# The second unit of each feed forward layer computed plain, in the other four PSUM banks, with its post-processing written behind the next unit

## The chip, the cores and the metric

The kernel runs on one core of a Trainium2 chip. The metric is the device time of one execution in microseconds, the median of three runs. Beside it stands the profile of one execution, taken by the hardware profiler; its span runs from the first to the last instruction.

## What is computed

One decoder layer on a residual x of 256 tokens by 2048 columns, in float32: half a SwiGLU layer, a mixer with two branches, half a second SwiGLU layer. Only the first and third steps are changed:

```python
def swiglu(h, w_gu, w_down):
    g, u = jnp.split(h @ w_gu, 2, axis=-1)
    return (jax.nn.silu(g) * u) @ w_down

x = x + 0.5 * swiglu(rms_norm(x, g_ffn1[l]), w_gu1[l], w_down1[l])
x = x + hybrid_mixer(rms_norm(x, g_mix[l]), ...)
x = x + 0.5 * swiglu(rms_norm(x, g_ffn2[l]), w_gu2[l], w_down2[l])
```

`w_gu` is 2048 by 11264 (5632 gate and 5632 up columns), `w_down` 5632 by 2048.

## The kernel before

**Split arithmetic.** Each float32 operand is held as two fp32r tiles, `hi` and `lo`, and a product is three matmuls: x hi by w hi, x hi by w lo, x lo by w hi. `split` makes the pair: ScalarE copies to `hi` (L98), VectorE subtracts to get `lo` (L99).

**Units.** A feed forward layer goes through its 11 units of 512 gate and 512 up columns in blocks of 4, 4 and 3 (`UNITS`). Behind each block its activations are multiplied with `w_down` in four column chunks (`dn`, n = 0 to 3, function `by_token`). A *plain* unit has 16 parts, one for each 128 rows of the weights; a part is 4 products (gate and up, two token halves of 128), which is 12 matmuls of 128x512. The other units follow `PLAN = "sppspspp"`: the 16 row blocks are taken as 8 pairs, and for an "s" pair the 8 products are replaced by 7 (Strassen's scheme in Winograd's form, `seven`), which come in four parts and need sums of the weights (`u`, L167 to L169, on VectorE), and sums of the activations, the *forms*. Three "s" pairs a unit save 9 matmuls out of 192.

**Normalisation.** The first unit works on x times the gains; each token's factor `rstd` is applied at the end (`direct`: ScalarE's silu with scale, L486, here called the *gate*, and VectorE's multiplication, L490, the *up*). The forms need activations that are normalised. `turn_into_forms` does that in place for one pair: L315 and L316 on VectorE, four small operations L320 to L323 if the pair is an "s", then a split back into `h` (L98, L99). Each FFN needs 8 such *turns*. The split back on ScalarE has to wait until TensorE has read the old `h`.

**PSUM.** There are eight banks: `ps_mm` has two tiles of two banks each, `ps_t` two tiles of one (tag "tr"), `ps_a` two of one ("sc", "po"). A plain unit has its four accumulators in `ps_mm`. A unit by plan has four of its accumulators there, and p5, p7, p6 and p1 in the other four banks. After the last "s" pair `gather` reads these four, and at the unit's end `combine` (L476 to L479) reads the two `ps_mm` tiles. A `dn` chunk takes one `ps_mm` tile; its `add` (L562) reads it into x.

**Order of the work.** All engines work in the order in which the program is written. `Feed.take` gives the next weight part and first writes the splits of the parts ahead: three pairs of buffers for any part, and two more from the pool `late` for parts of units whose plan is given. `pending` holds small steps, one of which is written behind each part; `posts` holds steps that are written at the end of a `take`, one each, or three when five are queued. `turns` are the transposes of a unit's activations (`transpose4`, into `ps_t`), then split into `act`. In the first FFN `NormOfColumns` computes the statistics from `xT` during unit 0: squares on ScalarE (`stats`, L350), their sum on GpSimd (L352), `sums`, `total`, `spread`, all put into `pending` by `start1`.

Behind the mixer stands the product with `w_o` in four chunks (`o`, `by_token`), whose `add` is L835, and which feeds the second FFN.

Of the kernel before, what the change touches and what calls it, by code (L numbers as in the profile page):

```python
# [12 lines left out]
F32 = mybir.dt.float32  # L13
F32R = mybir.dt.float32r
AF = mybir.ActivationFunctionType
# [4 lines left out]
P = 128  # L20
D = 2048
S = 256
TB = S // P
NKD = D // P
DFF = 5632
UNITS = (4, 4, 3)
PAIRS = NKD // 2
PLAN = "sppspspp"
HD = 64
NQ = 16  # L30
NKV = 4
# [9 lines left out]
NCH = 512  # L41
# [11 lines left out]
def hybrid_layer(ctx: ExitStack, tc: tile.TileContext, a: dict, out: bass.AP):  # L53
# [47 lines left out]
    def halves(cat, k0, k1):  # L101
        return cat[:, k0:k1, 0], cat[:, k0:k1, 1]

    def transpose4(srcs, name):

        pt = ps_t.tile([P, 2, S], F32, tag="tr", name=name)
# [9 lines left out]
    def run(queue, n=1):  # L116
        for _ in range(min(n, len(queue))):
            queue.pop(0)()
# [271 lines left out]
    def add_ffn(w_gu, w_down, first=None):  # L390
        u0 = 0
        for units in UNITS:
            for u in range(u0, u0 + units):
                hooks = dict(plan=PLAN if u else None)
                if first and u == 0:
                    cuts = [NCH, NCH] + [SUB] * 7
                    hooks = dict(cuts=cuts, on_fetch=first.fetch, on_split=first.parts)
# [17 lines left out]
    class Unit:  # L415


        def __init__(self, norm, fpool, late_pool):
            self.norm, self.fpool, self.pool = norm, fpool, late_pool
            self.begun = set()  # L420
            self.banks = {}

        def bank(self, name):

            if name in ("a0", "a1", "b0", "b1"):
                if name[0] not in self.banks:
                    self.banks[name[0]] = ps_mm.tile([P, 2, NCH], F32, tag="mm", name="gu")
                return self.banks[name[0]][:, int(name[1])]
            if name not in self.banks:
                pool, tag = dict(p1=(ps_t, "tr"), p6=(ps_t, "tr"), p5=(ps_a, "sc"), p7=(ps_a, "po"))[name]  # L430
                self.banks[name] = pool.tile([P, NCH], F32, tag=tag, name=name)
            return self.banks[name]
# [49 lines left out]

        def direct(self):
            g = self.g = self.fpool.tile([P, TB, NCH], F32, tag="g", name="g", bufs=2)
            for t in range(TB):
                nc.scalar.activation(  # L486
                    g[:, t], self.banks["ab"[t]][:, 0], AF.Silu, scale=self.norm.rstd[:, t:t + 1]
                )
            for t in range(TB):
                nc.vector.scalar_tensor_tensor(  # L490
                    g[:, t], self.banks["ab"[t]][:, 1], self.norm.rstd[:, t:t + 1], g[:, t],
                    op0=ALU.mult, op1=ALU.mult,
                )

        def turns(self, act, k):

            def turn(j):
                pt = transpose4([self.g[:, t, 2 * P * j:2 * P * (j + 1)] for t in range(TB)], "at")
                posts.append(lambda: split(halves(act, k + 2 * j, k + 2 * j + 2), pt))

            return [lambda j=j: turn(j) for j in range(UKT // 2)]

    def ffn(norm, fpool, open_late, first=None, after=None, late=(), out_rows=None):
        late_pool = None if first else open_late()
        n_unit = 0
        for i, units in enumerate(UNITS):
# [1 line left out]
            act = fpool.tile([P, max(UNITS) * UKT, 2, S], F32R, tag="act", name="act")  # L508
            turns = []
            for u in range(units):  # L510
                unit = Unit(norm, fpool, late_pool)
                if n_unit == 0:
                    end = NKD * SUB
                    if first:
                        first()
                    col = w = 0
                    while col + w < end:
                        hi, lo, w, col = feed.take()
                        unit.plain(hi, lo, w, col, col + w == end)
                        run(pending)  # L520
                        if first and col + w == end - 2 * SUB:
                            late_pool = unit.pool = open_late()
                        if norm.spread_done and late_pool and 2 * (norm.turned + 1) * SUB <= col + w:
                            norm.turn_into_forms(norm.turned, late_pool)
                            norm.turned += 1
                    run(posts, len(posts))
                    unit.direct()
                else:
                    for p in range(PAIRS):
                        if norm.turned <= p:  # L530
                            norm.turn_into_forms(norm.turned, late_pool)
                            norm.turned += 1
                        if PLAN[p] == "s":
                            unit.seven(p, "s" not in PLAN[p + 1:])
                            if "s" not in PLAN[p + 1:]:
                                unit.gather()
                            continue
                        for j in range(2):
                            hi, lo, w, col = feed.take()
                            unit.plain(hi, lo, w, col, p == PAIRS - 1 and j == 1)  # L540
                            run(pending)
                            if norm.turned < PAIRS:
                                norm.turn_into_forms(norm.turned, late_pool)
                                norm.turned += 1
                            if p == PAIRS - 1 and j == 0:
                                run(turns, len(turns))
                    run(posts, len(posts))
                    unit.combine()
                run(turns, len(turns))
                turns = unit.turns(act, u * UKT)  # L550
                n_unit += 1
                if late:
                    late.pop(0)()
            pending.extend([lambda: None] * 2 + turns)
            for n in range(ND):
# [28 lines left out]
    with tc.tile_pool(name="ffn1", bufs=1) as fpool, ExitStack() as early, ExitStack() as later:  # L584
# [33 lines left out]
    with tc.tile_pool(name="mix", bufs=1) as mix:  # L618
# [300 lines left out]
```

## Time and profile before

| | |
|---|---|
| median of 3 runs | 2131.32 us (2130.17 to 2131.93) |
| profiled execution, its own time | 2131.02 us |
| its span | 2129.2 us |
| TensorE (matmul) busy | 2067.4 us, 97% |
| VectorE busy | 1513.2 us, 71% |
| ScalarE busy | 1027.3 us, 48% |
| GpSimd busy | 64.3 us, 3% |
| mean granted TensorE clock | 0.991 of full speed |

The busy time of TensorE is modelled from pipelined matmuls, so that 97% does not say that the array is at its peak. What counts is where matmuls don't follow each other: most of the span TensorE is busy without a break, and its breaks lie at the beginnings of the two feed forward layers and at the ends of blocks. Time outside the span is 1.8 us.

### The profile page before, as it was taken

The numbers are of one execution on the slowest core, as the hardware profiler recorded it, in microseconds if no ns is written. First come the engines' busy times: TensorE is split into PE (matmuls) and PEld (weight loads), VectorE is DVE, ScalarE is ACT, GpSimd is POOL, SyncE is SP. The second block draws the span as 40 slices with busy tenths as digits, with TensorE's granted clock in tenths as the row PEclk, the third lists the DMA queues.
The fourth block names the chain that finished last, engine by engine and source line by source line (L and its number), as shares of the span: only waits on it lengthen the run. The fifth ranks groups of instructions, "written<-read, shape, count | busy, mean of one in ns | idle before, by whom it ended". The sixth has DMA issues, their size and how long they took to land.

```text
span 2129.2 us, 24288 instructions
## 1 busy us (share of the span) xinstructions
PE 2067.4 (97%) x9560; PEld 1687.9 (79%) x9560; DVE 1513.2 (71%) x1669; ACT 1027.3 (48%) x1234; POOL 64.3 (3%) x55
## 2 busy tenths in 40 slices
PE   8799999999999999999999999979999999999999
PEld 7578778887788788877888888757878778787777
DVE  5888568885688654668666665588965888648874
ACT  5454445543455454455545444445543555434543
POOL 1000000000000000621000000000000000000000
PEclk9899999999999999999999999999999999999999
DMA  6355555554555455443555555434555545555454
GB/s 242 124 190 215 178 198 199 190 205 158 198 197 199 168 183 186 160 152 113 184 197 181 195 187 189 178 127 170 198 181 194 198 178 199 190 187 195 183 193 158
DMA packets 57939, 389.68 MB, mean 183 GB/s; under 512 B 6880, under 2 KB 8032, under 8 KB 11744
## 3 DMA queue, kind: packets, MB, share of 16 engines
q1 hardware_dynamic: 57680, 388.10, 50.2%
q8 instruction: 75, 1.23, 0.2%
q14 instruction: 40, 0.33, 0.0%
q10 hardware_dynamic: 144, 0.02, 0.0%
HBM read 386.00 MB, written 2.10 MB: 182 GB/s over the span
## 4 chain that ended last, share of the span: by engine, by line
PE 88%; DVE 6%; ACT 2%; issue 2%; POOL 1%; DMA 1%; SPq 0%; ACTq 0%; DVEq 0%; POOLq 0%
PE gu L437 10%; PE gu L438 10%; PE gu L436 10%; PE dn L221 8%; PE dn L223 8%; PE dn L222 7%; PE gate L243 5%; DVE lo L99 3%; PE yo L243 3%; PE gate L245 3%; PE p L436 2%; PE p L437 2%; PE p L438 2%; PE xc L243 2%; ACT hi L98 2%
## 5 line engine op out<-in xcount | busy, mean ns | idle before, releaser
L99 DVE TENSOR_TENSOR lo<-raw,hi 128x1024 fp32r<-128x1024 f32 (+1 forms) x729 | 868.6, 1203 | 525.0 <-ACT hi L98 517.5
L98 ACT CAST hi<-raw 128x1024 fp32r<-128x1024 f32 (+1 forms) x729 | 728.0, 1012 | 631.9 <-PE dn L223 253.0
L436 PE MATMUL gu<-hi,h 128*128 128x512 f32 x1048 | 418.7, 399 | 29.2 <-DVE g L490 8.1
L437 PE MATMUL gu<-lo,h 128*128 128x512 f32 x1048 | 417.3, 398 | 9.0 <-DVE lo L99 8.2
L438 PE MATMUL gu<-hi,h 128*128 128x512 f32 x1048 | 414.3, 395 | 0.0
L221 PE MATMUL dn<-hi,act 128*128 128x512 f32 x704 | 278.7, 396 | 8.8 <-DVE v L477 8.8
L223 PE MATMUL dn<-hi,act 128*128 128x512 f32 x704 | 276.2, 392 | 0.0
L222 PE MATMUL dn<-lo,act 128*128 128x512 f32 x704 | 273.8, 389 | 0.0
L436 PEld LDWEIGHTS gu<-hi,h 128*128 128x128 f32 x1048 | 198.9, 190 | 84.6 <-issue 12.8
L437 PEld LDWEIGHTS gu<-lo,h 128*128 128x128 f32 x1048 | 198.9, 190 | 61.7 <-DVE lo L99 19.4
L98 ACT CAST hi<-u 128x1024 fp32r<-128x1024 f32 x120 | 126.2, 1052 | 229.7 <-DVE u L167 183.2
L438 PEld LDWEIGHTS gu<-hi,h 128*128 128x128 f32 x1048 | 198.9, 190 | 45.1 <-DVE h L285 0.8
L243 PE MATMUL gate<-h,hi 128*128 128x512 f32 x512 | 179.2, 392 | 0.0
L221 PEld LDWEIGHTS dn<-hi,act 128*128 128x128 f32 x704 | 132.3, 188 | 37.4 <-issue 11.2
L223 PEld LDWEIGHTS dn<-hi,act 128*128 128x128 f32 x704 | 132.2, 188 | 30.2
L222 PEld LDWEIGHTS dn<-lo,act 128*128 128x128 f32 x704 | 132.2, 188 | 28.8
L99 DVE TENSOR_TENSOR lo<-u,hi 128x1024 fp32r<-128x1024 f32 x120 | 146.5, 1222 | 3.4 <-ACT hi L98 0.3
L245 PE MATMUL gate<-h,lo 128*128 128x256 f32 x480 | 134.4, 280 | 0.0
L243 PEld LDWEIGHTS gate<-h,hi 128*128 128x128 f32 x512 | 95.9, 187 | 20.6 <-issue 0.8
L243 PE MATMUL xc<-h,hi 128*128 128x512 f32 x256 | 93.4, 407 | 0.0
L245 PEld LDWEIGHTS gate<-h,lo 128*128 128x128 f32 x480 | 90.7, 189 | 0.7
L167 DVE TENSOR_TENSOR u<-raw 128x1024 f32<-128x1024 f32 x60 | 73.1, 1218 | 0.0
(198 smaller groups left out, 2364.8 us busy)
## 6 DMA issues: line engine op xcount, KB each, us to landing
raw<-in_w_gu SPq DMA_DIRECT2D x172, 1024.0 KB, 4.6
raw<-in_w_down SPq DMA_DIRECT2D x88, 1024.0 KB, 4.6
raw<-in_w_mix SPq DMA_DIRECT2D x56, 1024.0 KB, 5.0
raw<-in_w_o SPq DMA_DIRECT2D x16, 1024.0 KB, 4.7
raw<-in_w_qkv SPq DMA_DIRECT2D x12, 1024.0 KB, 4.7
raw<-in_w_oc SPq DMA_DIRECT2D x8, 1024.0 KB, 4.9
raw<-in_w_oa SPq DMA_DIRECT2D x8, 1024.0 KB, 4.7
raw<-in_w_gu SPq DMA_DIRECT2D x7, 512.0 KB, 6.6
```

The costliest lines, as they stand in the source:

```text
L98: nc.scalar.copy(dst[0], src)
L99: nc.vector.tensor_tensor(dst[1], src, dst[0].bitcast(F32), op=ALU.subtract)
L167: nc.vector.tensor_tensor(u[:, :2], b[:, 0:4:3], b[:, 1:2].broadcast_to([P, 2, NCH]), op=ALU.add)
L221: nc.tensor.matmul(ps[t], x[:, k, 0, ts], hi[:, js], start=k == 0, stop=False)
L222: nc.tensor.matmul(ps[t], x[:, k, 0, ts], lo[:, js], start=False, stop=False)
L223: nc.tensor.matmul(ps[t], x[:, k, 1, ts], hi[:, js], start=False, stop=k == kts - 1)
L243: nc.tensor.matmul(ps[:, b], whi, both, start=k == 0, stop=last)
L245: nc.tensor.matmul(ps[:, b, :S], wlo, x[:, k, 0], start=False, stop=False)
L436: nc.tensor.matmul(ps, x[0], hi, start=name not in self.begun, stop=False)
L437: nc.tensor.matmul(ps, x[0], lo, start=False, stop=False)
L438: nc.tensor.matmul(ps, x[1], hi, start=False, stop=last)
```

## The change

Units 0 and 1 of each FFN are plain (`PLAIN = 2`). Unit 1 has its accumulators in the four other banks (`other`), and the 8 turns stand among the parts of unit 1 instead of unit 0 (second FFN) or of unit 1 by plan (first FFN). Unit 0's gates and ups, which `direct` now returns as four steps, go into `posts`, behind parts of unit 1; its transposes go into `pending`, into a `ps_mm` tile ("wide"). Unit 1's gates and ups are written at its end, before unit 2. The parts of unit 0 may use the two additional buffers too. The first `dn` chunk of each block and the last `o` chunk accumulate in `ps_a`, and the `add` of a block's last `dn` chunk is written before the next block's first `take`. The statistics of the first FFN start one part later and end sooner.

```diff
+PLAIN = 2
-                hooks = dict(plan=PLAN if u else None)
+                hooks = dict(plan=PLAN if u >= PLAIN else "p" * PAIRS)
...
         def bank(self, name):
+            if self.other:
+                if name not in self.banks:
+                    pool, tag = dict(a0=(ps_a, "sc"), b0=(ps_a, "po"), a1=(ps_t, "tr"), b1=(ps_t, "tr"))[name]
+                    self.banks[name] = pool.tile([P, NCH], F32, tag=tag, name="gu")
+                return self.banks[name]
...
+            return [lambda t=t, f=f: f(t) for f in (gate, up) for t in range(TB)]
...
+        def turns(self, act, k, wide=False):
             def turn(j):
-                pt = transpose4([self.g[:, t, 2 * P * j:2 * P * (j + 1)] for t in range(TB)], "at")
+                if wide and j == 0:
+                    self.wide = ps_mm.tile([P, 2, 2, S], F32, tag="mm", name="at")
+                pt = transpose4(
+                    [self.g[:, t, 2 * P * j:2 * P * (j + 1)] for t in range(TB)], "at",
+                    self.wide[:, j] if wide else None,
+                )
...
-                unit = Unit(norm, fpool, late_pool)
-                if n_unit == 0:
+                unit = Unit(norm, fpool, late_pool, n_unit == 1)
+                if n_unit < PLAIN:
...
-                        if norm.spread_done and late_pool and 2 * (norm.turned + 1) * SUB <= col + w:
+                        if n_unit and 2 * (norm.turned + 1) * SUB <= col + w:
                             norm.turn_into_forms(norm.turned, late_pool)
                             norm.turned += 1
-                    run(posts, len(posts))
-                    unit.direct()
+                    posts.extend(unit.direct())
+                    if n_unit:
+                        run(posts, len(posts))
...
-                turns = unit.turns(act, u * UKT)
+                turns = unit.turns(act, u * UKT, n_unit == 0)
+                if n_unit == 0:
+                    pending.extend([lambda: None] * 5 + turns)
+                    turns = []
...
-                by_token(act, units * UKT, "dn", add, apart=final and n == ND - 1)
+                by_token(act, units * UKT, "dn", add, apart=n == 0 or final and n == ND - 1)
+            if not last:
+                run(posts, len(posts))
...
-                pending.extend((lambda c=c: norm1.stats(c), *[skip] * c))
-            pending[:0] = [skip] * 3
+                pending.extend((lambda c=c: norm1.stats(c), *[skip] * (c % 3)))
+            pending[:0] = [skip] * 4
...
-            by_token(m, NKD, "o", add)
+            by_token(m, NKD, "o", add, apart=n == ND - 1)
```

**First place, VectorE, second FFN, the first turn.** Before, it stands in unit 0 behind two splits, with one split of a part (`lo<-raw,hi`) behind each turn:

```order
L99 TENSOR_TENSOR lo<-raw,hi 128x1024 x2
L315 TENSOR_TENSOR rn<-h_9876 128x512
L316 TENSOR_TENSOR rn<-rn,rows_9877 128x512
L320 TENSOR_TENSOR rf<-rn 128x128
L321 TENSOR_TENSOR rn<-rn 128x128
L322 SCALAR_TENSOR_TENSOR rf<-rn 128x128
L323 TENSOR_TENSOR rf<-rn,rf 128x128
L99 TENSOR_TENSOR forms_10516<-rf,forms_10516 128x384
L99 TENSOR_TENSOR h_9876<-rn,h_9876 128x2x256
L99 TENSOR_TENSOR lo<-raw,hi 128x1024
L315 TENSOR_TENSOR rn<-h_9876 128x512
```

After, on the same engine, it stands behind fourteen splits, the last six of them unit 1's own:

```order
L100 TENSOR_TENSOR lo<-raw,hi 128x1024 x14
L317 TENSOR_TENSOR rn<-h_9841 128x512
L318 TENSOR_TENSOR rn<-rn,rows_9842 128x512
L322 TENSOR_TENSOR rf<-rn 128x128
L323 TENSOR_TENSOR rn<-rn 128x128
L324 SCALAR_TENSOR_TENSOR rf<-rn 128x128
L325 TENSOR_TENSOR rf<-rn,rf 128x128
L100 TENSOR_TENSOR forms_10703<-rf,forms_10703 128x384
L100 TENSOR_TENSOR h_9841<-rn,h_9841 128x2x256
L100 TENSOR_TENSOR lo<-raw,hi 128x1024
L499 SCALAR_TENSOR_TENSOR g<-gu,rs_y,g 128x512
L100 TENSOR_TENSOR lo<-raw,hi 128x1024
```

Two splits now stand behind each turn, and unit 0's ups (L499) between them.

**Second place, ScalarE, second FFN, the last turn.** Before, unit 0's gates (`g<-gu`) follow the last turn's `h<-rn` and a load of the function table:

```order
L98 CAST h_9876<-rn 128x2x256
L98 CAST hi<-raw 128x1024
L98 CAST hi<-raw 128x512
L98 CAST h_9876<-rn 128x2x256
L486 ACT_TABLE_LOAD
L486 ACTIVATE g<-gu,rs_y 128x512 x2
L98 CAST hi<-raw 128x1024 x4
```

After, unit 1's gates follow it, without a load; unit 2's first p5 accumulates in the bank that the first of them reads:

```order
L99 CAST h_9841<-rn 128x2x256
L99 CAST hi<-raw 128x1024
L99 CAST hi<-raw 128x512
L99 CAST h_9841<-rn 128x2x256
L494 ACTIVATE g<-gu,rs_y 128x512 x2
L99 CAST hi<-raw 128x1024 x4
```

The same sequence has moved from the end of unit 0 to the end of unit 1.

**Third place, VectorE, the end of the first block.** Before, the last chunk's `add` (`x_res<-dn`) stands behind a split that the next unit's first `take` writes:

```order
L99 TENSOR_TENSOR lo<-u,hi 128x1024 x2
L99 TENSOR_TENSOR lo<-raw,hi 128x1024
L99 TENSOR_TENSOR lo<-raw,hi 128x512
L99 TENSOR_TENSOR lo<-raw,hi 128x1024
L562 SCALAR_TENSOR_TENSOR x_res<-dn,x_res 128x512 x2
L99 TENSOR_TENSOR lo<-raw,hi 128x1024 x3
```

After, it stands before that split:

```order
L100 TENSOR_TENSOR lo<-u,hi 128x1024 x2
L100 TENSOR_TENSOR lo<-raw,hi 128x1024
L100 TENSOR_TENSOR lo<-raw,hi 128x512
L576 SCALAR_TENSOR_TENSOR x_res<-dn,x_res 128x512 x2
L100 TENSOR_TENSOR lo<-raw,hi 128x1024 x4
```

The one split that stood ahead of the `add` has gone behind it.

## Rows read from the trace of the kernel before

**Rows 1.** Windows of 20 us: busy of PE, PEld, DVE, ACT, POOL, clock, DMA

```profile
1420.00:1440.00 20.00, 10.85 (x45) 8.05 (x44) 15.91 (x22) 10.80 (x14) 0.00 (x0) 0.87 0.39 145
1460.00:1480.00 20.00, 20.00 (x91) 16.37 (x90) 18.22 (x21) 10.70 (x12) 0.00 (x0) 1.00 0.57 211
```

**Rows 2.** Waits of PE: us in total, times, longest us

```profile
PE dn L221 <- DVE v L477: 8.8, 6, 1.5
PE gu L436 <- DVE x_res L562: 3.8, 4, 1.0
```

**Rows 3.** Timeline of PE: start us, us, engine line op out<-in xcount [idle]

```profile
41.58 0.51 PE L437 MATMUL gu<-lo,h 128*128 128x512 f32 x1 [1.75 <-DVE lo L99]
...
57.32 0.60 PE L306 MATMUL spread<-diag,ones 128*128 128x128 f32 x4
...
127.16 0.39 PE L436 MATMUL p<-hi,forms 128*128 128x512 f32 x1
...
1371.53 0.39 PE L436 MATMUL gu<-hi,h 128*128 128x512 f32 x1
...
1375.28 0.50 PE L436 MATMUL gu<-hi,h 128*128 128x512 f32 x1 [2.90 <-DVE x_res L835]
...
1386.81 0.39 PE L437 MATMUL gu<-lo,h 128*128 128x512 f32 x1
...
1391.80 0.39 PE L438 MATMUL gu<-hi,h 128*128 128x512 f32 x1
...
1439.76 0.80 PE L436 MATMUL gu<-hi,h 128*128 128x512 f32 x1 [8.08 <-DVE g L490]
...
1444.62 0.63 PE L438 MATMUL p<-hi,h 128*128 128x512 f32 x1
...
1483.25 0.40 PE L436 MATMUL p<-hi,forms 128*128 128x512 f32 x1
```

**Rows 4.** Timeline of DVE: turns in the second FFN, then one split of `act`

```profile
1412.60 0.68 DVE L315 TENSOR_TENSOR rn<-h 128x512 f32<-128x512 f32 x1
...
1417.98 0.68 DVE L315 TENSOR_TENSOR rn<-h 128x512 f32<-128x512 f32 x1
...
1422.75 2.36 DVE L99 TENSOR_TENSOR lo<-raw,hi 128x1024 fp32r<-128x1024 f32 x2 [0.26 <-ACT hi L98]
1425.03 1.22 DVE L167 TENSOR_TENSOR u<-raw 128x1024 f32<-128x1024 f32 x1
...
1429.96 0.68 DVE L315 TENSOR_TENSOR rn<-h 128x512 f32<-128x512 f32 x1
...
1434.80 0.68 DVE L315 TENSOR_TENSOR rn<-h 128x512 f32<-128x512 f32 x1
...
1438.95 1.41 DVE L490 SCALAR_TENSOR_TENSOR g<-gu,rs_y,g 128x512 f32<-128x512 f32 x2 [1.31 <-ACT g L486]
...
1569.49 1.28 DVE L99 TENSOR_TENSOR act<-at,act 128x512 fp32r<-128x512 f32 x2
```

**Rows 5.** Timeline of ACT: end of unit 0, second FFN

```profile
1436.30 0.62 ACT L98 CAST h<-rn 128x512 fp32r<-128x512 f32 x1 [2.75 <-DVE rn L316]
1436.93 1.28 ACT L486 ACT_TABLE_LOAD   x1
1438.23 1.26 ACT L486 ACTIVATE g<-gu,rs_y 128x512 f32<-128x512 f32 x2
```

**Rows 6.** Page, costliest groups: line engine op, out<-in, count | busy us, mean ns | idle

```profile
L99 DVE TENSOR_TENSOR lo<-raw,hi 128x1024 fp32r<-128x1024 f32 (+1 forms) x729 | 868.6, 1203 | 525.0 <-ACT hi L98 517.5
L98 ACT CAST hi<-raw 128x1024 fp32r<-128x1024 f32 (+1 forms) x729 | 728.0, 1012 | 631.9 <-PE dn L223 253.0
```

**Rows 7.** Timeline of ACT: the last squares of the first FFN's statistics

```profile
36.88 1.06 ACT L350 ACTIVATE sq<-xT 128x1024 f32<-128x1024 f32 x1 [6.38 <-issue]
```

**Rows 8.** Timeline of PE: start of a block's `dn`, start of the next block

```profile
1572.36 0.47 PE L221 MATMUL dn<-hi,act 128*128 128x512 f32 x1 [1.47 <-DVE v L477]
...
1665.13 0.47 PE L436 MATMUL gu<-hi,h 128*128 128x512 f32 x1 [0.94 <-DVE x_res L562]
```

More of the change, by code (lines that the diff above doesn't have):

```diff
@@ L102, in halves, with transpose4 @@
         return cat[:, k0:k1, 0], cat[:, k0:k1, 1]
-    def transpose4(srcs, name):
-        pt = ps_t.tile([P, 2, S], F32, tag="tr", name=name)
+    def transpose4(srcs, name, pt=None):
+        if pt is None:
+            pt = ps_t.tile([P, 2, S], F32, tag="tr", name=name)
         for j in range(2):
@@ L393, in add_ffn @@
             for u in range(u0, u0 + units):
-                hooks = dict(plan=PLAN if u else None)
+                hooks = dict(plan=PLAN if u >= PLAIN else "p" * PAIRS)
                 if first and u == 0:
                     cuts = [NCH, NCH] + [SUB] * 7
-                    hooks = dict(cuts=cuts, on_fetch=first.fetch, on_split=first.parts)
+                    hooks.update(cuts=cuts, on_fetch=first.fetch, on_split=first.parts)
                 feed.add(w_gu[u], NKD * SUB, **hooks)
@@ L415, in hybrid_layer, with __init__ @@
     class Unit:
-        def __init__(self, norm, fpool, late_pool):
-            self.norm, self.fpool, self.pool = norm, fpool, late_pool
+        def __init__(self, norm, fpool, late_pool, other=False):
+            self.norm, self.fpool, self.pool, self.other = norm, fpool, late_pool, other
             self.begun = set()
@@ L484, in direct, with gate, up @@
             g = self.g = self.fpool.tile([P, TB, NCH], F32, tag="g", name="g", bufs=2)
-            for t in range(TB):
+            def gate(t):
                 nc.scalar.activation(
-                    g[:, t], self.banks["ab"[t]][:, 0], AF.Silu, scale=self.norm.rstd[:, t:t + 1]
+                    g[:, t], self.bank("ab"[t] + "0"), AF.Silu, scale=self.norm.rstd[:, t:t + 1]
                 )
-            for t in range(TB):
+            def up(t):
                 nc.vector.scalar_tensor_tensor(
-                    g[:, t], self.banks["ab"[t]][:, 1], self.norm.rstd[:, t:t + 1], g[:, t],
+                    g[:, t], self.bank("ab"[t] + "1"), self.norm.rstd[:, t:t + 1], g[:, t],
                     op0=ALU.mult, op1=ALU.mult,
                 )
-        def turns(self, act, k):
+            return [lambda t=t, f=f: f(t) for f in (gate, up) for t in range(TB)]
+        def turns(self, act, k, wide=False):
             def turn(j):
-                pt = transpose4([self.g[:, t, 2 * P * j:2 * P * (j + 1)] for t in range(TB)], "at")
+                if wide and j == 0:
[4 more added lines that the diff above has]
+                )
                 posts.append(lambda: split(halves(act, k + 2 * j, k + 2 * j + 2), pt))
@@ L510, in ffn @@
             for u in range(units):
-                unit = Unit(norm, fpool, late_pool)
-                if n_unit == 0:
+                unit = Unit(norm, fpool, late_pool, n_unit == 1)
+                if n_unit < PLAIN:
                     end = NKD * SUB
-                    if first:
+                    if first and n_unit == 0:
                         first()
@@ L520, in ffn @@
                         run(pending)
-                        if first and col + w == end - 2 * SUB:
+                        if first and n_unit == 0 and col + w == end - 2 * SUB:
                             late_pool = unit.pool = open_late()
-                        if norm.spread_done and late_pool and 2 * (norm.turned + 1) * SUB <= col + w:
+                        if n_unit and 2 * (norm.turned + 1) * SUB <= col + w:
                             norm.turn_into_forms(norm.turned, late_pool)
                             norm.turned += 1
-                    run(posts, len(posts))
-                    unit.direct()
+                    posts.extend(unit.direct())
+                    if n_unit:
+                        run(posts, len(posts))
                 else:
                     for p in range(PAIRS):
-                        if norm.turned <= p:
-                            norm.turn_into_forms(norm.turned, late_pool)
-                            norm.turned += 1
                         if PLAN[p] == "s":
@@ L541, in ffn @@
                             run(pending)
-                            if norm.turned < PAIRS:
-                                norm.turn_into_forms(norm.turned, late_pool)
-                                norm.turned += 1
                             if p == PAIRS - 1 and j == 0:
```

## The prediction

> **What bounds the kernel now.** I read the windows first. Where the layer runs by plan, TensorE fills its window: 20.00 of 20 us at clock 1.00, with VectorE at 18.22 [rows 1]. Where the turns stand, TensorE has 10.85 of 20 us, VectorE 15.91, and the clock is 0.87. So the second is a stretch in which TensorE waits for VectorE and ScalarE, and only there, and at block ends, can the time change.
>
> The waits of TensorE give the block ends: six waits of `dn` for `combine`, 8.8 us together, and four of a new unit for the last `add`, 3.8 us [rows 2].
>
> The timeline of TensorE gives the two beginnings as absolute times, which is all the sum needs [rows 3]. First FFN: after a wait for a split TensorE goes on at 41.58, unit 0 ends at 57.32 (the `spread` stands behind it), and unit 2's first matmul starts at 127.16. Second FFN: unit 0 starts at 1371.53, waits 2.90 us for the last `o` chunk's `add`, waits 8.08 us for unit 0's up at 1439.76, and unit 2 starts at 1483.25. Between 1386.81 and 1391.80 stand 22 steps from matmul to matmul, so the pitch at full clock is 4.99 / 22 = 0.227 us: 2.72 us for a part of 12, 43.6 us for a plain unit. Behind the long wait, 11 steps take 1444.62 - 1439.76 = 4.86 us, 0.44 us each: the lower of the two clock levels, 1.2 instead of 2.4 GHz. That costs 4.86 - 2.50 = 2.4 us.
>
> **Unit 1, the main term.** What is written into unit 1 is 16 splits (six of them ahead of the first turn), 8 turns, unit 0's two ups and two `act` splits, and unit 2's first sums and splits. I lay VectorE's time end to end with the distances between its rows in the second FFN, where the same turns follow each other today [rows 4]; the waits for ScalarE inside are part of them.
> - A turn of a "p" pair with two splits behind it: 1417.98 - 1412.60 = 5.38 us. An "s" pair with two: 1425.03 - 1417.98 = 7.05. An "s" pair up to its first split: 1422.75 - 1417.98 = 4.77.
> - Unit 2's sums `u` and two splits of them: 1429.96 - 1425.03 = 4.93. The turn behind them with one long and one short split: 1434.80 - 1429.96 = 4.84.
> - The last turn, from its first operation to the end of a gate [rows 4, 5]: 1436.30 - 1434.80 = 1.50, the cast of `h` 0.62, one gate 1.26 / 2 = 0.63: 2.75. Today's load of the function table (1.28) drops out here, since unit 0's gates have loaded it by then.
> - The two ups 1.41, the two `act` splits 1.28 [rows 4].
>
> Pairs 0, 3 and 5 are "s". The chain from the first turn: pair 0 and ups 7.05 + 1.41; pair 1, 5.38; pair 2 and `act` 5.38 + 1.28; pair 3, 7.05; pair 4, 5.38; pair 5 and sums 4.77 + 4.93; pair 6, 4.84; pair 7 and gate 2.75. Sum 50.2 us.
>
> When does it begin? The first turn stands behind part 5's split. That split needs the buffer of part 0, free 2.72 us after the unit's start; ScalarE has meanwhile a cast, the table load (1.28) and a gate (0.63) to do, then casts part 5 and VectorE subtracts. With 1.05 and 1.2 us for a cast and a subtraction (estimates from the groups' means of 1.012 and 1.203, which mix in shorter ones [rows 6]) this is 1.05 + 1.28 + 0.63 + 1.05 + 1.2 = 5.2, with handovers 5.4 us. So unit 1's first gate ends 5.4 + 50.2 = 55.6 us after the unit's start.
>
> TensorE needs 43.6 us for the unit and some 0.7 for unit 0's eight transposes. Up to there nothing holds it: turn p needs part 2p + 1 read, its two splits are for parts 2p + 6 and 2p + 7, and by the same chain part 15's split ends near 39 us, when TensorE starts it at 41.6. But unit 2's first p5 uses the bank that unit 1's first gate reads, and that gate stands on ScalarE behind the last turn's cast. **All the lag of VectorE comes out at this one place**: TensorE waits 55.6 - 44.3 = 11.3 us, and then I add 2.4 us for the low clock, as behind the 8.08 us wait. The nine added matmuls of each unit 1 (2.0 us) lie inside this wait. Unit 2 starts in effect at 58.0 us.
>
> Bounds for 55.6 + 2.4: if the turns came through without lag, TensorE would wait only for the cast and the gate, about 1.5 us: 45.8. Above: today's nearest stretch, eight turns and a unit by plan in the first FFN, 127.16 - 57.32 = 69.8. I take 58.0, because it is built from rows of the same instructions in the same order.
>
> On this point the Trainium skill (TensorE: Matmul & The Clock Gate, Seeing it yourself) warns that the clock gate has been seen stuck at a quarter rate for more than 50 us. By it each of the two waits would cost some 37 us or more, and the kernel would be slower than before. In this trace the clock was back within 4.86 us [rows 3], and no run here shows it stuck.
>
> **Unit 0.** Second FFN: no turns in it, and the last `o` chunk is in other banks, so the 2.90 us wait goes. 43.6 us and some 1.2 for two transposes and the `spread`; the `add` now stands behind two more splits, since five buffers are filled first, for which I take a wait of 0.7 us ahead of the transposes. It ends at 1371.5 + 45.5 = 1417.0. Unit 2 starts in effect at 1417.0 + 58.0 = 1475.0 instead of 1483.25: **8.2 us gained**.
>
> First FFN: ScalarE's last square waited 6.38 us for `xT` up to 36.88 [rows 7], and the casts of the next parts stood behind it; TensorE's 1.75 us at 41.58 [rows 3] is what that led to. One more part is now split ahead of each square, so weight buffers come free, and the transfers with the last pieces of `xT` are issued, some 2 to 3 us sooner. Against it, the sum of the squares is read two parts sooner, and may hold TensorE about 2 us. I take 4 us, between -2 and 6. Unit 0 ends at 53.3, unit 2 starts at 111.3 instead of 127.16: **15.9 us gained**.
>
> **Block ends.** The first `dn` chunk finds its banks read by `gather` four parts earlier, so its wait (1.47 us at 1572.36 [rows 8]) goes, six times: 8.8 us. The transposes behind its third part, 8.2 us after the unit's end, still find `g` ready: `combine`, silu and the multiplication end about 5 us after it. A block's `add` is ahead of the next unit's split, 1.3 us after the last `dn` matmul, and the bank is wanted 12 matmuls (2.7 us) after it: 3.8 us more [rows 2], one of them the 0.94 at 1665.13 [rows 8]. The split that it passes covers a part 10 us ahead. With about 0.1 us at each of ten restarts (the first matmul takes 0.47): **13.6 us**.
>
> **The sum.** 15.9 + 8.2 + 13.6 = 37.7 us off the profiled execution's own time of 2131.0 (span 2129.2 and 1.8 around it): 2093.3. The median of the runs is 0.3 above that execution: **2093.6**.
>
> **The rivals.**
> - *The lag stays hidden.* If VectorE and ScalarE keep up (casts overlapping better than today's rows show), unit 2 starts at 45.8 instead of 58.0: 2 x 12.2 = 24.4 less, 2069. Against it: in the window with the turns VectorE is busy 15.91 of 20 us though only 45 matmuls are recorded [rows 1]. 8%.
> - *The turns cost what they cost, wherever they stand.* Both stretches run as the first FFN's does today, 69.8 us from unit to unit: 2 x 11.8 more, 2117, little more than the block ends gained. For it: all VectorE work of the turns is still there. Against it: the rows show the turns faster than that in the second FFN. 11%.
> - *Slower: the clock stays low behind the new wait.* The wait of 11.3 us is longer than any in these rows. If TensorE ran all 183 matmuls of unit 2 at 0.44 us, it would lose 183 x 0.213 = 39 us instead of 2.4, in both FFNs: 2094 + 73 = 2167. It decides from a loss of 18.9 us beyond the 2.4 in each, some 89 slow matmuls more than the 11 seen. Against it, the clock came back within those 11 although the unit behind was of the same kind. 4%.
> - *No change*: the block ends gain, and the units give it back (2131 within 0.2%, which is 4 us and about what a measurement of this kernel can tell from no change). It needs some 7 us more in each unit 1 than the 69.8 us stretch already takes. 2%.
>
> **The numbers.** My forecast has 75%, between about 2080 and 2107 (3 us either way in each unit 1's chain, 4 in the statistics, 1 to 2 in each low-clock stretch). The range 2074 to 2108 leaves out the rivals' times and some of the forecast's edges. Faster by over 0.2%: 0.93; within: 0.02; slower: 0.05.
>
> **What would show it.** Right: unit 0 of the second FFN without a break; one break of 8 to 14 us ahead of unit 2's first p5 in each FFN, released by ScalarE's `g`, clock low behind it; no wait of `dn` for `v`, none for `x_res` at block ends; unit 0 of the first FFN ending between 51 and 56. Wrong: waits for `lo` inside unit 1 (then the chain is longer than its rows), a break under 4 us ahead of unit 2 (the first rival), or new waits inside units 2 and 3, where VectorE at 18.22 of 20 has little to spare.

## The result and the profile after

| | before | after |
|---|---|---|
| median | 2131.62 us (2130.17 to 2131.93, 4 runs) | 2095.15 us (2093.73 to 2096.36, 4 runs) |
| profiled execution: own time, span | 2131.02, 2129.2 us | 2095.90, 2094.1 us |
| ratio, 95% interval | | 0.983 [0.9813, 0.9847] |

The changed kernel is faster by 36.5 us; 2093.6 was forecast. In the code of after, what was L436 to L438 is now L443 to L445, the split is L99 (ScalarE) and L100 (VectorE), a turn begins at L317, gates and ups are L494 and L499, the transposes L111.

The waits of TensorE after (total us, times, longest us), where [rows 2] had `dn` and `x_res`:

```profile
PE p L443 <- ACT g L494: 11.2, 2, 5.6
PE at L111 <- DVE act L100: 8.4, 2, 4.2
...
PE gu L443 <- DVE v L486: 1.7, 8, 0.2
PE ssq L363 <- DVE acc L358: 1.6, 1, 1.6
...
PE xt L111 <- DVE x_res L851: 0.2, 1, 0.2
```

Both waits of the block ends are gone. In their place stand two waits in each feed forward layer: the forecast one ahead of unit 2's p5 (`p`), and one that was not forecast, of unit 0's transposes (`at`). TensorE's timeline of after, answering [rows 3] and [rows 8], says where:

```profile
41.69 0.58 PE L363 MATMUL ssq<-ones,acc 128*128 128x1 f32 x4 [1.63 <-DVE acc L358]
...
55.20 0.39 PE L443 MATMUL gu<-hi,h 128*128 128x512 f32 x1
...
79.29 0.66 PE L111 MATMUL at<-ident,g 128*128 128x128 f32 x4 [4.17 <-DVE act L100]
...
111.83 0.80 PE L443 MATMUL p<-hi,forms 128*128 128x512 f32 x1 [5.58 <-ACT g L494]
...
201.41 0.39 PE L223 MATMUL dn<-hi,act 128*128 128x512 f32 x1
...
1350.90 0.39 PE L443 MATMUL gu<-hi,h 128*128 128x512 f32 x1
...
1396.88 0.39 PE L443 MATMUL gu<-hi,h 128*128 128x512 f32 x1
...
1413.39 0.60 PE L111 MATMUL at<-ident,g 128*128 128x128 f32 x4
...
1420.98 0.66 PE L111 MATMUL at<-ident,g 128*128 128x128 f32 x4 [4.24 <-DVE act L100]
1421.39 0.60 PE L443 MATMUL gu<-hi,h 128*128 128x512 f32 x1
...
1425.12 0.39 PE L443 MATMUL gu<-hi,h 128*128 128x512 f32 x1
...
1453.60 0.80 PE L443 MATMUL p<-hi,forms 128*128 128x512 f32 x1 [5.59 <-ACT g L494]
...
1459.24 0.39 PE L444 MATMUL gu<-lo,h 128*128 128x512 f32 x1
...
1543.06 0.39 PE L223 MATMUL dn<-hi,act 128*128 128x512 f32 x1
```

Unit 1 starts at 55.20 and 1396.88, unit 2 at 111.83 and 1453.60: 56.6 and 56.7 us later, where 55.6 was forecast. The first `dn` matmuls (201.41, 1543.06) have no wait any more. The windows show the two slow patches of the second layer in the clock column. [rows 1] has the beginning of the only one before, around the long wait: 0.87 in the window from 1420.

```profile
1420.00:1440.00 20.00, 19.02 (x78) 15.54 (x79) 15.91 (x26) 7.44 (x11) 0.00 (x0) 0.91 0.41 147
1440.00:1460.00 20.00, 14.41 (x52) 11.29 (x52) 15.52 (x19) 9.12 (x12) 0.00 (x0) 0.83 0.18 66
1460.00:1480.00 20.00, 20.00 (x89) 16.23 (x88) 15.47 (x16) 9.46 (x11) 0.00 (x0) 1.00 0.56 208
```

Where the 35.1 us between the two profiled executions lie (first rows of each stretch, before and after):

| stretch | before | after | gained |
|---|---|---|---|
| start to first `dn` | 216.45 | 201.41 | 15.0, of which 1.5 the `dn` wait |
| first `dn` to second layer | 216.45 to 1371.53: 1155.1 | 201.41 to 1350.90: 1149.5 | 5.6 |
| second layer to its first `dn` | 1371.53 to 1572.36: 200.8 | 1350.90 to 1543.06: 192.2 | 8.7, of which 1.5 the `dn` wait |
| first `dn` of it to the end | 1572.36 to 2129.2: 556.8 | 1543.06 to 2094.1: 551.0 | 5.8 |

So the beginnings gained 13.6 and 7.2 us, and the block ends 5.6 + 5.8 + 2.9 (the two `dn` waits) = 14.3.

### The profile page after: what moved, and what is told of

The parts are those of the page before. It is cut to its first block, busy times and chain, and to the rows that moved or that the text cites. A ratio compares the mean times of both kernels' runs of the same rounds, so it can differ in the third digit from the quotient of the medians.

```text
span 2094.1 us, 24270 instructions
## 1 busy us (share of the span) xinstructions
PE 2060.8 (98%) x9578; PEld 1691.7 (81%) x9578; DVE 1478.0 (71%) x1625; ACT 1017.8 (49%) x1222; POOL 64.6 (3%) x55
## 3 DMA queue, kind: packets, MB, share of 16 engines
q1 hardware_dynamic: 57680, 388.10, 51.3%
## 4 chain that ended last, share of the span: by engine, by line
PE 92%; DVE 4%; ACT 1%; POOL 1%; issue 1%; DMA 0%; SPq 0%; ACTq 0%; DVEq 0%; POOLq 0%
PE gu L444 11%; PE gu L445 11%; PE gu L443 11%; PE dn L225 8%; PE dn L224 8%; PE dn L223 8%; PE gate L245 6%; PE yo L245 3%; PE gate L247 3%; PE p L443 2%; PE p L444 2%; PE p L445 2%; PE xc L245 2%; DVE lo L100 2%; PE bg L245 2%; PE o L223 1%
## 5 line engine op out<-in xcount | busy, mean ns | idle before, releaser
L100 DVE TENSOR_TENSOR lo<-raw,hi 128x1024 fp32r<-128x1024 f32 (+1 forms) x729 | 872.0, 1208 | 526.5 <-ACT hi L99 519.4
L99 ACT CAST hi<-raw 128x1024 fp32r<-128x1024 f32 (+1 forms) x729 | 731.2, 1016 | 632.2 <-PE dn L225 236.3
L443 PE MATMUL gu<-hi,h 128*128 128x512 f32 x1084 | 430.2, 397 | 2.1 <-DVE v L486 1.7
L444 PE MATMUL gu<-lo,h 128*128 128x512 f32 x1084 | 428.7, 395 | 1.1 <-DVE lo L100 0.6
L445 PE MATMUL gu<-hi,h 128*128 128x512 f32 x1084 | 427.2, 394 | 0.0
L443 PEld LDWEIGHTS gu<-hi,h 128*128 128x128 f32 x1084 | 205.3, 189 | 52.5 <-issue 6.1
L444 PEld LDWEIGHTS gu<-lo,h 128*128 128x128 f32 x1084 | 205.1, 189 | 51.3 <-DVE lo L100 6.9
L445 PEld LDWEIGHTS gu<-hi,h 128*128 128x128 f32 x1084 | 204.7, 189 | 45.9 <-DVE h L287 0.4
L99 ACT CAST hi<-u 128x1024 fp32r<-128x1024 f32 x108 | 113.6, 1052 | 203.4 <-DVE u L169 159.2
L100 DVE TENSOR_TENSOR lo<-u,hi 128x1024 fp32r<-128x1024 f32 x108 | 131.8, 1222 | 3.2 <-ACT hi L99 0.3
L247 PE MATMUL xc<-h,lo 128*128 128x256 f32 x240 | 67.8, 282 | 0.0
```

Of the source, the lines that this page charges most:

```text
L99: nc.scalar.copy(dst[0], src)
L100: nc.vector.tensor_tensor(dst[1], src, dst[0].bitcast(F32), op=ALU.subtract)
L247: nc.tensor.matmul(ps[:, b, :S], wlo, x[:, k, 0], start=False, stop=False)
L443: nc.tensor.matmul(ps, x[0], hi, start=name not in self.begun, stop=False)
L444: nc.tensor.matmul(ps, x[0], lo, start=False, stop=False)
L445: nc.tensor.matmul(ps, x[1], hi, start=False, stop=last)
```

## The experiments

Theory 1 is the prediction's: VectorE's and ScalarE's chain through unit 1 sets when unit 2 starts, and TensorE gets the whole lag ahead of p5. The rivals say that each wait is a loss of its own, that the lag is only moved, or that the edits pay only together. The last column is the second layer in the profiled execution, from its first `gu` to its first `dn` matmul. The first layer's beginning is less comparable: seven of these kernels are the same program up to the `spread`, and yet it stands anywhere from 49.30 us (after) to 52.00 (two tiles).

| kernel | median | ratio to before, interval | second layer |
|---|---|---|---|
| after | 2095.15 | 0.983 [0.9813, 0.9847] | 192.2 |
| block ends alone | 2113.35 | 0.991 [0.9896, 0.9923] | 1362.77 to 1558.74: 196.0 |
| two tiles | 2091.01 | 0.9807 [0.9792, 0.9821] | 1351.17 to 1540.61: 189.4 |
| late turns | 2081.79 | 0.9762 [0.9747, 0.9776] | 1344.79 to 1530.08: 185.3 |
| longer turns | 2106.09 | 0.988 [0.9863, 0.9896] | 1356.07 to 1552.60: 196.5 |
| later sums | 2093.44 | 0.9818 [0.9803, 0.9833] | 1348.63 to 1542.12: 193.5 |
| same banks | 2088.08 | 0.9796 [0.9782, 0.9809] | 1349.77 to 1539.30: 189.5 |
| written at once | 2088.43 | 0.9793 [0.978, 0.9807] | 1347.19 to 1535.45: 188.3 |
| combination | 2075.94 | 0.9736 [0.9723, 0.9749] | 1341.45 to 1524.48: 183.0 |
| combination, same banks | 2075.07 | 0.9733 [0.9719, 0.9746] | 1340.91 to 1522.43: 181.5 |
| plain first pair | 2069.41 | 0.9702 [0.9688, 0.9715] | 1340.06 to 1518.46: 178.4 |
| combination, plain first pair | 2066.29 | 0.9688 [0.9675, 0.9701] | 1334.86 to 1513.28: 178.4 |
| the same, pair turned in two steps | 2070.18 | 0.9713 [0.97, 0.9726] | 1338.37 to 1518.97: 180.6 |

**Block ends alone.** The kernel before with three edits:

```diff
-                by_token(act, units * UKT, "dn", add, apart=final and n == ND - 1)
+                by_token(act, units * UKT, "dn", add, apart=n == 0 or final and n == ND - 1)
+            if not last:
+                run(posts, len(posts))
...
-            by_token(m, NKD, "o", add)
+            by_token(m, NKD, "o", add, apart=n == ND - 1)
```

> The kernel before with nothing but the edits at the ends of blocks: the first dn chunk of each block and the last o chunk in the other banks, and the add of a block's last dn chunk written ahead of the next block's first parts. Theory 1 (these edits act by themselves): no wait of dn for v and none of gu for x_res; 13.6 us by the prediction's sum for the block ends and up to 2.9 for the o chunk, 14 to 17 us faster than before, 2114 to 2117. Rival (they only pay together with the plain second unit, because buffers and banks are bound otherwise): less than 8 us, above 2123.

Measured 18.8 us faster than before in the same runs (2132.10), somewhat above the 14 to 17. The stretches from the first `dn` to the second layer (213.56 to 1362.77: 1149.2) and from the next to the end (1558.74 to 2109.8: 551.1) are as short as after. So half of the change's gain does not need the plain second unit. What the other edits add, in the profiled executions, is 213.56 - 201.41 = 12.2 us in the first layer and 196.0 - 192.2 = 3.8 in the second. Of the 7.2 us that the second layer's beginning gained, nearly 3 thus belong to the last `o` chunk's new place. The beginnings keep their waits: TensorE still stands for unit 0's up, as in [rows 3].

```profile
PE gu L436 <- DVE g L490: 8.1, 1, 8.1
PE gu L437 <- DVE lo L99: 8.1, 11, 1.7
```

**Two tiles.** The changed kernel, where the second transposes of unit 0 no longer share a PSUM tile with the first:

```diff
-                if wide and j == 0:
+                if wide:
...
-                    self.wide[:, j] if wide else None,
+                    self.wide[:, 0] if wide else None,
```

> The changed kernel, with each of unit 0's two transposes in a PSUM tile of its own instead of halves of one. Theory 1 (VectorE's and ScalarE's chain through unit 1 sets when unit 2 starts): the wait of 4.2 us for the act split goes in both feed forward layers, but the wait ahead of unit 2's first p5 grows from 5.6 to about 9; the gain is the low-clock stretch behind the first wait (about 2.2 us) and up to 1 us of the chain, 2 to 3 us in each layer: some 6 us less than the changed kernel, about 2089. Rival (each wait is a loss of its own): the wait ahead of p5 stays at 5.6, and 4.2 + 2.2 us are gained twice: about 13 us less, 2082.

Faster by 4.1 us by the medians (the intervals overlap); the second layer by 2.7. The wait for `act` is gone and the wait for the gate has grown from 5.6 to 10.0 us:

```profile
PE p L443 <- ACT g L494: 20.0, 2, 10.0
```

Unit 1 begins at 1397.15, and p5 starts here:

```profile
1452.30 0.80 PE L443 MATMUL p<-hi,forms 128*128 128x512 f32 x1 [10.00 <-ACT g L494]
```

Of the 4.2 us and the 1.7 us of low clock behind them, 4.4 us were paid a second time at p5. What was gained in the second layer is 1.6 us of the chain (55.15 instead of 56.72 us from unit 1's start to p5) and 1.1 us because fewer matmuls were slow behind p5 (7 steps instead of 13). So the low-clock patch behind the first wait, which the expectation counted as the gain, was absorbed like that wait. Theory 1 holds, the rival's 13 us don't. Why the transposes waited is told by VectorE's rows in the changed kernel: the first transposes stand at 1413.39, but VectorE comes to their split only at 1420.24, behind a turn and the splits around it, and the second ones could not start while the tile was unread.

```profile
1419.09 1.23 DVE L100 TENSOR_TENSOR lo<-raw,hi 128x1024 fp32r<-128x1024 f32 x1 [0.26 <-ACT hi L99]
1420.24 0.68 DVE L100 TENSOR_TENSOR act<-at,act 128x512 fp32r<-128x512 f32 x1
```

**Late turns.** Turns 6 and 7 written among unit 2's parts:

```diff
-                        if n_unit and 2 * (norm.turned + 1) * SUB <= col + w:
+                        if n_unit and norm.turned < 6 and 2 * (norm.turned + 1) * SUB <= col + w:
...
+                            if norm.turned < PAIRS and j == 1:
+                                norm.turn_into_forms(norm.turned, late_pool)
+                                norm.turned += 1
```

> The changed kernel, with the last two of the eight turns of each feed forward layer written among the parts of unit 2 instead of unit 1. Theory 1 (the chain of all eight turns delays unit 1's gate, and the whole lag comes out ahead of unit 2's first p5): the chain is about 10 us shorter, 5 us of which are more than TensorE still has to wait; the wait of 5.6 us and the low clock behind it (2.5) go, and unit 2 starts 6 to 8 us sooner in each layer: 11 to 15 us less than the changed kernel, 2080 to 2084, a little less if unit 2 then waits for splits. Rival (the lag is only moved): the same loss shows up as waits inside unit 2 or at its end, and the time stays at 2095 within 4.

2081.8, 13.4 us less than after. No wait ahead of p5 is left; the `act` one stays as it was:

```profile
PE at L111 <- DVE act L100: 8.4, 2, 4.2
PE qp L111 <- POOL qall L693: 3.2, 1, 3.2
PE ssq L363 <- DVE acc L358: 2.2, 1, 2.2
```

The lag is not moved into unit 2, which has room for two turns without a new wait of more than 0.3 us: the second layer is 6.9 us shorter.

**Longer turns.** The first addition of each turn stands twice:

```diff
             nc.vector.tensor_tensor(t, h[:, :, 0].bitcast(F32), h[:, :, 1].bitcast(F32), op=ALU.add)
+            nc.vector.tensor_tensor(t, h[:, :, 0].bitcast(F32), h[:, :, 1].bitcast(F32), op=ALU.add)
```

> The changed kernel, with VectorE's first addition of each turn done twice (same result), 16 additional instructions of about 0.7 us. Theory 1 (VectorE's work in the turns comes out in full as a later start of unit 2): 8 x 0.7 = 5.8 us in each feed forward layer, 11 to 12 us more than the changed kernel, about 2107, seen as a longer wait ahead of unit 2's p5. Rival (VectorE waits for ScalarE in the turns, so that its own work is in part hidden): 0 to 6 us more, below 2101.

2106.1, 10.9 us more for 16 instructions of 0.68 us, or 10.9 us of VectorE: it comes out in full. In the profiled execution p5 comes 5.1 and 5.6 us later behind unit 1's start; the second layer is only 4.4 us longer, since fewer matmuls are slow behind p5 (1.2 us less lost). Both waits grow, `act` by 2.2 us in each layer, p5 by 3.1 in the first and 2.8 in the second:

```profile
PE p L444 <- ACT g L495: 17.1, 2, 8.7
PE at L111 <- DVE act L100: 12.8, 2, 6.4
```

**Later sums.** The statistics' sums two parts later:

```diff
-            pending.extend((norm1.sums, norm1.total, lambda: None, norm1.spread))
+            pending.extend((skip, skip, norm1.sums, norm1.total, lambda: None, norm1.spread))
```

> The changed kernel, with the sum of the squares of the first feed forward layer read by TensorE two parts later. Theory 1 (the statistics are read before GpSimd's and VectorE's last addition is done, and TensorE stands): the wait of 1.6 us at 41.7 us goes and so do the slow matmuls behind it (about 2 us): 3.5 us less than the changed kernel, near 2091.5, and unit 0 ends near 51.5 instead of 55.2. Rival (the spread and with it unit 1's first turn come later by as much, or unit 2's start hangs on VectorE's chain, which begins when it did): less than 1 us.

Inconclusive. The 1.6 us wait is gone from the list of waits, but the median is 1.7 us lower with intervals that overlap, and unit 2's p5 stands at 111.51 instead of 111.83. Between 3.5 and less than 1 it doesn't decide, since the early part of the program differs by up to 2.7 us from execution to execution (the `spread` rows above).

**Same banks.** Unit 1 in the usual tiles, unit 0's steps written at once:

```diff
-                unit = Unit(norm, fpool, late_pool, n_unit == 1)
+                unit = Unit(norm, fpool, late_pool)
...
-                    if n_unit:
-                        run(posts, len(posts))
+                    run(posts, len(posts))
...
-                turns = unit.turns(act, u * UKT, n_unit == 0)
+                turns = unit.turns(act, u * UKT)
```

> The changed kernel, with unit 1 in the same banks as unit 0, unit 0's gates and ups run at once and its transposes in the usual small tile. Theory 1 (the other banks are what lets unit 1 start without waiting for unit 0's post-processing): TensorE waits about 4 to 5 us ahead of unit 1 in each feed forward layer and runs slow behind it, 5 to 7 us more each, in part taken back where the wait for the act split (4.2 us) goes: 6 to 14 us more than the changed kernel, 2101 to 2109. Rival (VectorE's chain through unit 1 binds anyway, so that it doesn't matter where TensorE waits): the wait ahead of unit 2 gets shorter by as much, and the time stays at 2095 within 4.

Both fail: it is 7.1 us faster than after. TensorE's timeline in the second layer:

```profile
1397.10 0.50 PE L443 MATMUL gu<-hi,h 128*128 128x512 f32 x1 [1.18 <-DVE g L499]
...
1442.22 0.39 PE L443 MATMUL p<-hi,forms 128*128 128x512 f32 x1
...
1451.64 0.80 PE L443 MATMUL gu<-hi,h 128*128 128x512 f32 x1 [7.19 <-DVE g L499]
```

Unit 1 waits only 1.18 us for unit 0's ups, not 4 to 5: neither engine has a turn to do at that point. At unit 2 p5 starts at once in the other banks, nine matmuls are done, and the lag comes out 7.19 us long at the first product in the usual tiles. This kernel changes two things and takes away the `act` wait too, so the next one parts them.

**Written at once.** Two tiles, with only the writing changed:

```diff
-                    if n_unit:
-                        run(posts, len(posts))
+                    run(posts, len(posts))
```

> The kernel with two tiles for unit 0's transposes, with unit 0's gates and ups written at once at its end instead of behind parts of unit 1; unit 1 keeps the four other banks. It is to part the two things that the kernel with the same banks changed together (2088.1 against 2091.0). Theory A (the other banks bring nothing, and neither does the later writing: the chain through unit 1 holds the same work either way): 2091 within 3, with a wait of some 9 to 10 us ahead of unit 2's p5. Theory B (the two ups between the turns hold the turns up): the chain is shorter, the wait ahead of p5 is 8 or less, and the time 2087 or less.

2088.4, between the two theories: 2.6 us below two tiles with overlapping intervals, the wait ahead of p5 down from 10.0 to 8.5 us. In the second layer VectorE does the two ups (1.41 us) before the first turn, in time in which it waits for casts anyway; written behind parts they stand inside the chain, two tiles' first turn starting no sooner (51.3 us after the layer's first matmul against 51.2):

```profile
1393.74 1.41 DVE L499 SCALAR_TENSOR_TENSOR g<-gu,rs_y,g 128x512 f32<-128x512 f32 x2 [0.78 <-ACT g L494]
1395.25 1.23 DVE L100 TENSOR_TENSOR lo<-raw,hi 128x1024 fp32r<-128x1024 f32 x1
1397.20 1.23 DVE L100 TENSOR_TENSOR lo<-raw,hi 128x1024 fp32r<-128x1024 f32 x1 [0.72 <-ACT hi L99]
1398.34 0.68 DVE L317 TENSOR_TENSOR rn<-h 128x512 f32<-128x512 f32 x1
```

Beside it, same banks (2088.1) shows no use of the four other banks for unit 1 that the medians could tell.

**Combination** of two tiles, late turns and later sums, and the **combination with the same banks** in place of two tiles:

> The changed kernel with three edits together: unit 0's transposes in tiles of their own, the last two turns in unit 2, the sums of the statistics two parts later. If VectorE's chain is what is left, the three gains add up: both waits and the low-clock stretches behind them go, 8 to 10 us in each feed forward layer, and 3.5 us at the start: 2073 to 2078. If they hide one another: the best of the three alone, 2081 or more.

> The kernel with the same banks for unit 1, together with the last two turns in unit 2 and the statistics' sums two parts later. Theory A (the banks only decide at which matmul the lag comes out, at p5 or nine matmuls later at the first product in the usual tiles, and cost 1.2 to 1.6 us ahead of unit 1 instead): within 3 of the combination with the other banks, 2073 to 2079. Theory B (the other banks hide nothing and p5 first is a loss): 2070 or less.

2075.9 and 2075.1: the gains add up, and the banks again make no difference that can be told. In the first of them only one of the two waits is gone, where both were expected to go: ahead of p5 3.6 us remain in the first layer and 3.3 in the second.

**Plain first pair.** Two tiles, and unit 2 opens with a plain pair:

```diff
-                hooks = dict(plan=PLAN if u >= PLAIN else "p" * PAIRS)
+                hooks = dict(plan=PLAN if u > PLAIN else ("p" + PLAN[1:] if u == PLAIN else "p" * PAIRS))
...
-                        if PLAN[p] == "s":
+                        if PLAN[p] == "s" and (p or n_unit > PLAIN):
```

Here unit 2 multiplies that pair with activations in which the turn has put a difference in place of one quarter, so this part of the sum is not the reference's; the amount of work is right.

> The kernel with two tiles for the transposes, with the first pair of unit 2 plain instead of by Strassen's scheme, so that unit 2 opens with products in banks that unit 1's gates don't read; it first needs one of those three pairs (72 matmuls, 16 us) later. Three matmuls more in each feed forward layer (0.7 us), and no sums of weights for that pair (2.6 us of VectorE less in unit 1). Theory 1 (the lag of VectorE is a loss only because unit 2's p5 needs the bank of unit 1's gate, and five parts are split ahead): the 10 us wait and the low clock behind it (about 2) go, less 0.7: 11 us in each layer, 2068 to 2072. Rival (the lag is VectorE's own, and comes out a few parts later as waits for lo): at most the 2.6 us of the sums in each, 2085 or more.

2069.4, as theory 1 gave it, 21.6 us less than two tiles. The windows that held the long waits have none and the full clock:

```profile
100.00:120.00 20.00, 20.00 (x88) 16.23 (x88) 17.94 (x20) 11.19 (x15) 0.00 (x0) 1.00 0.53 184
1440.00:1460.00 20.00, 20.00 (x88) 16.32 (x87) 19.07 (x21) 12.30 (x14) 0.00 (x0) 1.00 0.47 174
```

The first p5 and unit 1's gates, on TensorE and on ScalarE:

```profile
1447.55 0.39 PE L443 MATMUL p<-hi,forms 128*128 128x512 f32 x1
```

```profile
1438.61 1.26 ACT L494 ACTIVATE g<-gu,rs_y 128x512 f32<-128x512 f32 x2
```

Unit 2 began 72 matmuls before that p5, at 1431.02; the first gate still ends 8.2 us after that, at 1438.61 + 0.63 (two tiles: 10.0), but 8.3 us before p5 wants the bank. So the lag is there, less 1.8 us, where the missing sums are 2.6 us of work, and costs nothing. It was the place at which it met TensorE that made it a loss.

**All together, and the pair turned in two steps.** The last kernel computes the whole layer; the one before it has the difference just told.

```diff
+            if scale:
...
-            if PLAN[p] == "s":
+            if forms and PLAN[p] == "s":
...
+                            norm.turn_into_forms(norm.turned, late_pool, forms=norm.turned > 0)
...
+                            elif n_unit == PLAIN and p == 4 and j == 1:
+                                norm.turn_into_forms(0, late_pool, scale=False)
```

> All that helped together: two tiles for the transposes, the first pair of unit 2 plain, the last two turns in unit 2, the statistics' sums two parts later. If the wait ahead of unit 2's p5 (3.3 to 3.6 us) and the low clock behind it (about 2) are all that is left of the beginnings, 2 x 4.7 us less than the combination without the plain pair: 2065 to 2068. If VectorE's load in unit 2 (19 of 20 us) now sets the pace there: 2073 to 2078.

> The combination with the plain first pair in unit 2, with that pair's turn split in two: in unit 1 it is only scaled, and its forms are made in unit 2, behind the pair's use (one more addition, four small operations and a split back, some 3.1 us of VectorE, while unit 1's first turn gets shorter by about 1.8). If VectorE has room for it in unit 2 (18 of 20 us busy there, with five parts split ahead): 2066 within 3, no wait of more than half a microsecond at the beginnings of the two feed forward layers. If not: waits for lo or forms in unit 2 or at the start of unit 3, up to 3 us in each layer, 2069 to 2073.

2066.3 and 2070.2. Late turns and later sums add nothing to the plain first pair that can be told: the intervals overlap, and the second layer takes 178.4 us with and without them. With the lag off TensorE's path, a shorter chain has nothing left to gain. The added turn in unit 2 brings the second branch of the last expectation, 2.2 us more in the second layer, in part as longer waits of unit 3's first products for unit 2's `combine`:

```profile
PE gu L444 <- DVE v L487: 1.9, 8, 0.3
PE gu L444 <- DVE v L485: 1.7, 2, 0.8
```

At 2070.2 it is the fastest kernel here that computes the reference, 25.0 us below the changed kernel by the medians, ratio to before 0.9713 [0.97, 0.9726].

## Why the prediction was right

The total was right, 2093.6 against 2095.15, and so was the mechanism. That it came so near is in part luck: as listed below, the terms missed by 5.3 us one way and by 2.7 the other, and the profiled execution lies 0.8 us above the median where 0.3 below was assumed.

- **The chain through unit 1.** Forecast: gate done 55.6 us after unit 1's start. In the kernel with two tiles, where nothing else holds TensorE, p5 starts 1452.30 - 1397.15 = 55.15 us after it, with a wait of 10.0 where 11.3 was forecast. The first turn starts 5.4 us after unit 1, as forecast, and from turn to turn no piece of the chain is off by more than 0.3 us, so this is no sum of errors that cancel. The wait is shorter than forecast mainly because TensorE took 45.15 us for unit 1 and the transposes, not 44.3. Longer turns showed that VectorE's time goes into the chain one to one.
- **The step that failed** is "up to there nothing holds it". Unit 0's two transposes were costed at their work alone; the second waits 4.2 us for VectorE to split the first out of the shared tile. So the one break of 8 to 14 us that was named as a sign of being right did not come as such: there are two, of 4.2 and 5.6 us. It cost little because it took from the wait at p5, but made the chain 1.6 us longer (56.7 against 55.15) and brought a second low-clock patch: from 1421.39 to 1425.12 stand 9 steps, 3.73 us where 2.04 would do, 1.7 lost. Behind p5, 13 steps from 1453.60 to 1459.24 took 5.64 instead of 2.95 us, 2.7 lost. The 2.4 forecast was read one matmul short: the one at 1444.62 [rows 3] is itself still slow (0.63 us), and the clock is back only behind it. Unit 2 starts in effect 56.7 + 2.7 = 59.4 us after unit 1, not 58.0, and unit 0 took 46.0 us instead of 45.5.
- **What the sum left out.** Those two misses would leave the second layer 6.3 us of its 8.2; it gained 7.2. Before, unit 2's first products waited for unit 1's `combine` and lost about 0.7 us by it. A plain unit 1 has no `combine`, and two of these waits are gone in the lists of before and after (the other 0.2 us are the slow restart behind the old `dn` wait):

```profile
PE gu L436 <- DVE v L479: 2.1, 10, 0.3
PE gu L443 <- DVE v L486: 1.7, 8, 0.2
```

- **The statistics** were sized at 4 us, between -2 and 6. Unit 0 ended at 55.2 instead of 53.3: the wait of 1.63 us that the text allowed for came, with slow matmuls behind it. With 1.5 more in unit 1, and about 1 us of the same short waits gone, this makes the first layer's 13.6 instead of 15.9. The start scatters, and no kernel had the change without the new order of the statistics, so how much this term brought stays open to some 2 us.
- **The block ends** gave 14.3, forecast 13.6, and give them alone too.
- **The rivals.** The turns at 69.8 us did not come, nor a hidden lag. The clock came back behind every wait at the beginnings, in the changed kernel at the latest after 14 steps (111.83 to 117.86). The Trainium skill's warning of a gate stuck for more than 50 us (TensorE: Matmul & The Clock Gate, Seeing it yourself) is not borne out by any run here.

What the prediction took as given and the experiments did not bear out: it said of the other banks only that unit 2's p5 needs one, and costed the later writing of unit 0's steps inside the chain without asking what they cost at once. Done at once they are out of the chain. With the usual banks TensorE then waits for them at unit 1's start, 1.2 and 1.6 us in the kernel with the same banks; the combination with the same banks is nevertheless as fast by the medians. So two parts of the change, the other banks and the later writing, brought nothing that these runs can tell.

## What to carry to other kernels

Here the lag of the late engines cost nothing until TensorE needed something from them. Find that one place, and see whether other work can stand ahead of it (72 plain matmuls here took a 10 us wait away) before making the late engine faster. Two results that shared a tile here shared its release, so that a late reader of the first held the second. Before post-processing is spread behind later work, look whether its engines are idle at the moment it becomes ready.

## What the runs showed that was not expected

The number of slow matmuls behind a wait did not follow the wait's length: 14 steps behind 5.58 us and 13 behind 5.59 after, but 10 and 7 behind the two waits of 10.0 us in two tiles (the second from 1452.30 to 1455.39, 3.09 us). A wait of 1.63 us was followed by slow matmuls, one of 2.90 us before (1375.28 [rows 3]) by none, and the one of 1.18 us in the kernel with the same banks by none. So the same second layer can differ by over 1 us between kernels that don't touch it (192.2 after, 193.5 with later sums).
